# Neighbourhood projections in 512 columns, gates moved beside the first attention, queries in 512 and 256 columns

## The chip, the cores and the metric

The kernel runs on one core of a Trainium2 chip. The metric is the device time of one execution in microseconds; lower is better. The engines of the core are TensorE (PE in the views: matmuls; PEld are its weight loads), VectorE (DVE), ScalarE (ACT), GpSimd (POOL) and SyncE (SP, which here only issues loads). They run side by side, each takes its instructions in the order in which the built program holds them, and they wait for one another through semaphores.

## The reference

A trunk of two layers with shared weights over 256 context and 256 latent tokens of width 1024, all in float32. In each layer, from a normed and modulated h, one product gives everything that the two attention branches need:

```python
p = h @ w_in                       # 1024 x 4640
gate_logits, c_q, c_kv, k_r, na = p split by columns
mq = rms_norm(rms_norm(c_q) @ w_uq)          # 8 heads x 96
k_nope, mv = rms_norm(c_kv) @ w_ukv          # 8 heads x (64 + 64)
mk = rms_norm(concat(k_nope, k_r))           # 8 heads x 96
nq, nk, nv = rms_norm(na[0]), rms_norm(na[1]), na[2]   # 8 heads x 64 each
y_mla = attention(mq, mk, mv)                # dense
y_na  = attention(nq, nk, nv) over a window of the grid (with a bias) and the context
g = sigmoid(gate_logits)                     # 2 x 1024
x = x + gt1 * ((g[:1024] * (y_mla @ w_mla_o) + g[1024:] * (y_na @ w_na_o)) @ w_out)
x = x + gt2 * relu(h2 @ w_ff1)**2 @ w_ff2
```

The modulations (shift, scale and gate of both halves) are `silu(c) @ w_ada`, a product of one or two rows. In the last layer the context tokens are only needed as keys and values, so the queries and all that follows have two blocks of 128 tokens instead of four.

## The kernel before

**Products.** A float32 product is three matmuls of the type fp32r (`mm3`, L100 to L103): each operand is split into a high part and the remainder, and high·high, high·low and low·high are added in one PSUM bank. Weights come from HBM into a tile `raw` of 128 x 1024 (five buffers, `wraw`, L116 to L118, issued by SP). ScalarE copies the high part (`whi`, L130) and VectorE subtracts it for the low part (`wlo`, L131); both have three buffers. PSUM has eight banks of 512 columns, named A (two), B (three), C (two) and D (one).

**Two forms of projection.** `proj_a` has the weights stationary: 128 output columns in a pass over 512 tokens (256 in the last layer). It makes the 16 gate chunks (`gates`). `proj_b` has the activations stationary and the weights moving: N output columns for 128 tokens. It makes the queries (`w_uq`: 288, 288 and 192 columns, three, three and two heads), the keys and values (`w_ukv`, twice 512 columns) and the neighbourhood projections (`chunk_na`, two halves of 256 columns for each of keys, queries and values, two blocks of tokens in the halves of one bank A).

**The order.** The program is written in one order, and a scheduler moves instructions of each engine by their readiness and by priorities that follow the written order; what it made of it is fixed when the kernel is built. In a layer: queries, keys and values of MLA; their norms and rotary parts on GpSimd (`q_stat`, `k_stat`, `q_fin`, `k_fin`); `gates(NG0[l], "B")`, six chunks in layer 0 and eight in layer 1; then the MLA attention, head by head (`prep_mla`: transposes L780 of the queries and L785 of the keys; scores; softmax on VectorE and ScalarE; transposes of P, L871; products with the values, L886 and L891). The neighbourhood projections are written behind the MLA attention, but the scheduler runs many of their matmuls between those of the attention, where these wait for the softmax. The neighbourhood attention follows, again with matmuls of later products in between, and the rest of the gates.

**The side job.** `ada_side` works out modulations on VectorE: for each of eight k it loads a row block of `w_ada` into a `raw` tile and adds it, times one value per partition, to an accumulator of 128 x 1024 for each of two rows (L251 for the first k, L255 for the others); transposes and reductions (L266, L267) follow, and L273 on TensorE adds up the partitions. It is a generator. Each call of `step()` runs one more piece of it, and the calls stand in `proj_a` (one after each chunk), in `chunk_na` and at the ends of stages (`step(99)`, the rest). In layer 0 the accumulators of its second use (`acc_v`) are allocated under the tag "v" with one buffer, under which `mv`, the values of the MLA attention, stand too.

**The bias.** The tables of the neighbourhood bias are loaded by SP, and GpSimd adds a mask (L816). `issue_after(q_end.ins)` has it stand behind the last rotary operation of the queries.

Of the kernel before, what the change touches and what calls it, by code (L numbers as in the profile page):

```python
# [14 lines left out]
KD = 8  # L15
# [6 lines left out]
NH = 8  # L22
# [23 lines left out]
def trunk(ctx: ExitStack, tc, t):  # L46
# [10 lines left out]
    def ps(tag):  # L57
        return pp.tile([128, 512], F32, tag="ps" + tag, name="ps" + tag, bufs=BANKS[tag])
# [406 lines left out]
    for l in range(DEPTH):  # L465
# [92 lines left out]

        turn = [0]

        def proj_b(load, nk, act_h, act_l, toks, N, evac, banks=None):

            tiles = [load(i) for i in range(nk)]
            total = sum(len(x[2]) for x in tiles)
            for p0 in range(0, len(toks), 2):
                pair = toks[p0:p0 + 2]
                if banks == "one":
                    o = ps("A")
                    outs = [o[:, i * N:(i + 1) * N] for i in range(2)]
                else:  # L570
                    turn[0] += 1
                    outs = [ps(b)[:, :N] for b in (banks[p0 // 2] if banks else ("AA", "BB")[turn[0] % 2])]
                parts = [list(zip(outs, pair))] if banks != "one" else [[x] for x in zip(outs, pair)]
                for part in parts:
                    n = 0
                    for wh, wl, ks in tiles:
                        for j, k in enumerate(ks):
                            for o, tk in part:
                                cs = slice(tk * 128, (tk + 1) * 128)
                                mm3(o, act_h(k)[:, cs], act_l(k)[:, cs], wh[:, j], wl[:, j], n == 0, n == total - 1)  # L580
                            n += 1
# [136 lines left out]
            nc.gpsimd.tensor_tensor(out=krz[:, t:t + 2, :], in0=z,  # L718
                                    in1=rk[:, t:t + 2].unsqueeze(2).to_broadcast([128, 2, NH]), op=ALU.mult)

        for h0, n in ((0, 3), (3, 3), (6, 2)):
            def evac(tk, o):
                dst = mq[:, tk, h0:h0 + n, :]
                nc.scalar.activation(out=dst, in_=o.rearrange("p (h d) -> p h d", h=n), func=AF.Copy)
                head_ss(qrs[:, tk, h0:h0 + n], dst, n, QK, rq[:, tk - q0:tk - q0 + 1])
                if h0 == 6 and tk % 2:
# [21 lines left out]
        def k_fin(tk):  # L748
            z = mk[:, tk, :, 0:NOPE]
            nc.gpsimd.tensor_tensor(out=z, in0=z, in1=krz[:, tk, :].unsqueeze(2).to_broadcast([128, NH, NOPE]),  # L750
                                    op=ALU.mult)
            nc.gpsimd.tensor_tensor(out=mk[:, tk, :, NOPE:QK], in0=kr[:, tk, :].unsqueeze(1).to_broadcast([128, NH, RD]),
                                    in1=krr[:, tk, :].unsqueeze(2).to_broadcast([128, NH, RD]), op=ALU.mult)
# [41 lines left out]
        def prep_na(hp):  # L795
            cs = slice(2 * hp * HD, (2 * hp + 2) * HD)
            o = ps("C")
            for tk in range(q0, 4):
                nc.tensor.transpose(o[:, tk * 128:(tk + 1) * 128], nqk[:, tk, cs], rev if tk >= 2 else ident)
            qh, ql = qk_tile(TQ), qk_tile(TQ)  # L800
            split_ps(qh, ql, o[:, c_q], gcn[:, l:l + 1])
            o = ps("C")
            for tk in range(4):
                nc.tensor.transpose(o[:, tk * 128:(tk + 1) * 128], nqk[:, 4 + tk, cs], ident)
            kh, kl = qk_tile(), qk_tile()
            split_ps(kh, kl, o)
            biases = []
            for h in (2 * hp, 2 * hp + 1):
                bias = ap.tile([128, 2, ROWS, GW], F32, tag="bias", name="bias", bufs=3 + l)
                for row in range(ROWS):  # L810
                    src = bass.AP(tensor=t["rpb"].tensor, offset=(l * NH + h) * RPB + (7 - row) * RW + 15 - (GW - 1),
                                  ap=[[1, GW], [RW, ROWS], [1, GW]])
                    pr = (row % 2) * 64
                    nc.sync.dma_start(out=bias[pr:pr + 64, row // 2], in_=src)
                with tc.issue_after(q_end.ins):
                    nc.gpsimd.tensor_tensor(out=bias.rearrange("p a i j -> p (a i) j"),  # L816
                                            in0=bias.rearrange("p a i j -> p (a i) j"),
                                            in1=wmask.unsqueeze(1).to_broadcast([128, 2 * ROWS, GW]), op=ALU.add)
                biases.append(bias)
            return qh, ql, kh, kl, biases  # L820
# [141 lines left out]

        nrs = ap.tile([128, 8, NH], F32, name="nrs")

        def chunk_na(part, half, toks):
            def evac(tk, o):
                cs = slice(half * 256, (half + 1) * 256)
                if part == 2:
                    nc.scalar.activation(out=nv[:, tk, cs], in_=o, func=AF.Copy)
                    return  # L970
                i = 4 * part + tk
                nc.scalar.activation(out=nqk[:, i, cs], in_=o, func=AF.Copy)
                head_ss(nrs[:, i, half * 4:half * 4 + 4], nqk[:, i, cs].rearrange("p (h d) -> p h d", h=4), 4, HD)
                if half == 1:
                    fin_r(nrs[:, i, :], nrs[:, i, :], HD)
                    z = nqk[:, i, :].rearrange("p (h d) -> p h d", h=NH)
                    nc.gpsimd.tensor_tensor(out=z, in0=z, in1=nrs[:, i, :].unsqueeze(2).to_broadcast([128, NH, HD]),
                                            op=ALU.mult)
# [331 lines left out]
```

## Time and profile before

| | |
|---|---|
| median of three runs | 1305.12 us (1301.83, 1305.12, 1305.75) |
| profiled execution: time, span | 1301.52 us, 1299.7 us |
| TensorE busy | 1267.2 us, 97% |
| VectorE busy | 914.2 us, 70% |
| ScalarE busy | 582.4 us, 45% |
| GpSimd busy | 264.2 us, 20% |
| granted TensorE clock, mean | 0.997 |

The matmuls are pipelined: one is listed from its start to its modelled end, so its own duration (0.28 us for 256 columns) is longer than the time to the start of the next. What one costs is the time from start to start. The span leaves out what lies around the program (1.8 us here).

### The profile page before, as it was taken

The numbers are of one execution on the slowest core, as the hardware profiler recorded it, in microseconds if no ns is written. First come the engines' busy times: TensorE is split into PE (matmuls) and PEld (weight loads), VectorE is DVE, ScalarE is ACT, GpSimd is POOL, SyncE is SP. The second block draws the span as 40 slices with busy tenths as digits, with TensorE's granted clock in tenths as the row PEclk, the third lists the DMA queues.
The fourth block names the chain that finished last, engine by engine and source line by source line (L and its number), as shares of the span: only waits on it lengthen the run. The fifth ranks groups of instructions, "written<-read, shape, count | busy, mean of one in ns | idle before, by whom it ended". The sixth has DMA issues, their size and how long they took to land.

```text
span 1299.7 us, 20369 instructions
## 1 busy us (share of the span) xinstructions
PE 1267.2 (97%) x7831; PEld 1090.3 (84%) x7831; DVE 914.2 (70%) x1547; ACT 582.4 (45%) x1054; POOL 264.2 (20%) x258
## 2 busy tenths in 40 slices
PE   7999999999999999999999999999999989999997
PEld 5698878986787898888778888998889779999896
DVE  4558987588985579898897744766763868665553
ACT  4455277346423243422322313565663645555452
POOL 0318403401014003210201200019031112121011
PEclk9999999999999999999999999999999999999999
DMA  9855710464486326566588732487114657646652
GB/s 295 290 112 155 219 33 20 130 172 57 129 281 226 98 67 204 155 192 193 177 290 262 208 96 77 131 190 213 55 50 120 129 185 200 176 157 189 192 188 87
DMA packets 241857, 208.01 MB, mean 160 GB/s; under 512 B 24464, under 2 KB 220816, under 8 KB 241376
## 3 DMA queue, kind: packets, MB, share of 16 engines
q1 hardware_dynamic: 231728, 190.16, 50.7%
q10 hardware_dynamic: 9520, 16.29, 3.5%
q8 instruction: 61, 1.00, 0.3%
q0 software_dynamic: 512, 0.27, 0.1%
q14 instruction: 36, 0.29, 0.1%
HBM read 195.15 MB, written 11.53 MB: 159 GB/s over the span
## 4 chain that ended last, share of the span: by engine, by line
PE 52%; DVE 4%; DMA 3%; issue 2%; POOL 2%; ACT 2%; SPq 0%; POOLq 0%; ACTq 0%; DVEq 0%
PE psB L101 6%; PE psB L102 6%; PE psB L103 6%; PE psA L103 6%; PE psA L101 6%; PE psA L102 6%; PE psC L103 4%; PE psC L101 4%; PE psC L102 4%; DVE wlo L131 2%; ACT whi L130 1%; PE psD L891 1%; DMA raw<-in_w_na_o_dram 1%; PE psC L871 1%; DMA raw<-in_w_ukv_dram 1%
## 5 line engine op out<-in xcount | busy, mean ns | idle before, releaser
L131 DVE TENSOR_TENSOR wlo<-raw,whi 128x1024 fp32r<-128x1024 f32 (+3 forms) x252 | 312.2, 1240 | 171.5 <-ACT whi L130 170.5
L130 ACT ACTIVATE whi<-raw 128x1024 fp32r<-128x1024 f32 (+3 forms) x252 | 260.8, 1035 | 357.8 <-PE psB L102 98.1
L255 DVE SCALAR_TENSOR_TENSOR ada<-raw,silu,ada 128x1024 f32<-128x1024 f32 (+1 forms) x126 | 160.7, 1310 | 0.5
L101 PE MATMUL psA<-whi,h 128*128 128x256 f32 (+2 forms) x408 | 120.4, 295 | 0.5 <-ACT h L345 0.4
L103 PE MATMUL psA<-whi,h 128*128 128x256 f32 (+2 forms) x408 | 120.3, 295 | 0.0
L102 PE MATMUL psA<-wlo,h 128*128 128x256 f32 (+2 forms) x408 | 120.2, 295 | 0.0
L102 PE MATMUL psB<-h,whi 128*128 128x256 f32 (+1 forms) x272 | 91.9, 338 | 0.0
L101 PE MATMUL psB<-h,whi 128*128 128x256 f32 (+1 forms) x272 | 91.7, 338 | 0.0
L103 PE MATMUL psB<-h,wlo 128*128 128x256 f32 (+1 forms) x272 | 91.6, 337 | 0.0
L101 PE MATMUL psA<-h,whi 128*128 128x512 f32 (+1 forms) x248 | 87.6, 354 | 1.2 <-ACT h L345 1.1
L102 PE MATMUL psA<-h,whi 128*128 128x512 f32 (+1 forms) x248 | 87.3, 352 | 0.2 <-DVE h L347 0.2
L103 PE MATMUL psA<-h,wlo 128*128 128x512 f32 (+1 forms) x248 | 87.1, 351 | 0.0
L101 PEld LDWEIGHTS psA<-whi,h 128*128 128x128 f32 x408 | 77.9, 191 | 2.8 <-ACT h L345 0.9
L102 PEld LDWEIGHTS psA<-wlo,h 128*128 128x128 f32 x408 | 77.9, 191 | 2.6 <-issue 0.8
L103 PEld LDWEIGHTS psA<-whi,h 128*128 128x128 f32 x408 | 77.8, 191 | 1.9
L1163 POOL TENSOR_TENSOR h<-s,h 128x512 fp32r<-128x512 f32 (+1 forms) x32 | 38.7, 1210 | 170.7 <-ACT h L1162 153.4
L1163 POOL TENSOR_TENSOR fl<-s,fa 128x512 fp32r<-128x512 f32 (+1 forms) x32 | 35.1, 1098 | 163.9 <-ACT fa L1162 163.9
L101 PE MATMUL psB<-G,whi 128*128 128x512 f32 (+2 forms) x192 | 66.7, 347 | 0.0
L103 PE MATMUL psB<-G,wlo 128*128 128x512 f32 (+2 forms) x192 | 66.2, 345 | 0.3 <-DVE wlo L131 0.3
L102 PE MATMUL psB<-G,whi 128*128 128x512 f32 (+2 forms) x192 | 66.4, 346 | 0.0
L101 PE MATMUL psC<-G,whi 128*128 128x258 f32 (+2 forms) x200 | 62.7, 313 | 0.0
L103 PE MATMUL psC<-G,wlo 128*128 128x258 f32 (+2 forms) x200 | 62.5, 312 | 0.0
(388 smaller groups left out, 3328.6 us busy)
## 6 DMA issues: line engine op xcount, KB each, us to landing
raw<-in_w_ff_dram SPq DMA_DIRECT2D x128, 512.0 KB, 4.1
raw<-in_w_ada_dram SPq DMA_DIRECT2D x80, 512.0 KB, 4.3
raw<-in_w_in_dram SPq DMA_DIRECT2D x62, 512.0 KB, 4.2
raw<-in_w_out_dram SPq DMA_DIRECT2D x16, 512.0 KB, 5.0
spare<-in_w_ada_dram SPq DMA_DIRECT2D x12, 512.0 KB, 8.5
xT_d<-xT SPq DMA_DIRECT2D x2, 2048.0 KB, 13.2
bias<-in_rpb_dram SPq DMA_DIRECT2D x64, 64.0 KB, 7.2
g_d<-g ACTq DMA_DIRECT2D x16, 256.0 KB, 4.2
```

The costliest lines, as they stand in the source:

```text
L101: nc.tensor.matmul(out, sh, mh, start=first, stop=False)
L102: nc.tensor.matmul(out, sh, ml, start=False, stop=False)
L103: nc.tensor.matmul(out, sl, mh, start=False, stop=last)
L130: nc.scalar.activation(out=hi, in_=src, func=AF.Copy)
L131: split[:] = [nc.vector.tensor_tensor(out=lo, in0=src, in1=hi.bitcast(F32), op=ALU.subtract).ins]
L255: nc.vector.scalar_tensor_tensor(out=a, in0=raw[:, c:c + w], scalar=sc, in1=a, op0=ALU.mult, op1=ALU.add)
L871: nc.tensor.transpose(o[:, kt * 256 + i * 128:kt * 256 + (i + 1) * 128], pt[:, (kp * 2 + kt) * 128:(kp * 2 + kt + 1) * 128], perm if K == ...
L891: mm = nc.tensor.matmul(yo[z * 64:(z + 1) * 64, oc], vsel(kt, 2 * hp + z), tr[kt // 2][:, kt % 2, :], start=kt == nkt - 1, stop=kt == 0, t ...
L1163: nc.gpsimd.tensor_tensor(out=al[:, f, :], in0=s[:, :TQ], in1=ah[:, f, :].bitcast(F32), op=ALU.subtract)
```

## The change

- Gates: `NG0 = (6, 8)` becomes `NG = ((5, 5), (4, 5))`. In front of the MLA attention five chunks are written in layer 0 and four in layer 1. Five further chunks are written behind the MLA attention, ahead of the neighbourhood projections, with bank A. The last six and seven follow the neighbourhood attention.
- Neighbourhood projections: `chunk_na` has its own loop instead of `proj_b`: 512 columns in one matmul, one bank for each block of 128 tokens (A, A, B, B; for the values A, A, D, B), weight tiles of two k instead of four. In the last layer the queries come first. `step()` is called after each weight tile of the values and twice after the queries.
- Queries: 512 and 256 columns instead of 288, 288 and 192. The head that straddles the border is summed with the second part.
- The mask additions stand behind the last key operation (`k_end`) instead of the last rotary operation of the queries.

```diff
-NG0 = (6, 8)
+NG = ((5, 5), (4, 5))
...
-        for h0, n in ((0, 3), (3, 3), (6, 2)):
+        for c0, n, h0, nh, kper in ((0, 512, 0, 5, 2), (512, 256, 5, 3, 3)):
             def evac(tk, o):
...
-            proj_b(loader(t["w_uq"][l], 0, h0 * QK, n * QK, 3, 2), 2, lambda k: ch[:, k], lambda k: cl[:, k],
-                   list(range(q0, 4)), n * QK, evac)
+            proj_b(loader(t["w_uq"][l], 0, c0, n, kper, 6 // kper), 6 // kper, lambda k: ch[:, k], lambda k: cl[:, k],
+                   list(range(q0, 4)), n, evac)
...
         for tk in range(4):
-            k_fin(tk)
+            k_end = k_fin(tk)
         for tk in range(q0, 4):
-            q_end = q_fin(tk)
-
-        gates(NG0[l], "B")
+            q_fin(tk)
+
+        gates(NG[l][0], "B")
         step(99)
...
-                with tc.issue_after(q_end.ins):
+                with tc.issue_after(k_end.ins):
                     nc.gpsimd.tensor_tensor(out=bias.rearrange("p a i j -> p (a i) j"),
...
-        def chunk_na(part, half, toks):
-            def evac(tk, o):
-                cs = slice(half * 256, (half + 1) * 256)
+        def chunk_na(part, toks, banks):
+
+            outs = [ps(b) for b in banks[:len(toks)]]
+            load = loader(w_in, 0, OFF_NA + part * 512, 512, 2, 4)
+            for i in range(4):
+                wh, wl, ks = load(i)
+                for j, k in enumerate(ks):
+                    for o, tk in zip(outs, toks):
+                        cs = slice(tk * 128, (tk + 1) * 128)
+                        mm3(o, hh[:, k, cs], hl[:, k, cs], wh[:, j], wl[:, j], k == 0, k == KD - 1)
                 if part == 2:
-                    nc.scalar.activation(out=nv[:, tk, cs], in_=o, func=AF.Copy)
-                    return
+                    step()
...
-            proj_b(loader(w_in, 0, OFF_NA + part * 512 + half * 256, 256, 4, 8), 2, H, Lo, toks, 256, evac, "one")
-            if (part, half) in ((0, 1), (2, 0), (2, 1)):
+            if part == 0:
                 step(2)
...
             side.append(ada_side(((0, 4, (0, 1)), (0, 3, (0, 1))), acc_v))
-        for part in (1, 0, 2):
-            for half in range(2):
-                chunk_na(part, half, list(range(q0, 4)) if part == 0 else [0, 1, 2, 3])
+        gates(NG[l][1])
+
+        for part, banks in ((0, "AA"), (1, "AABB"), (2, "AADB")) if last else ((1, "AABB"), (0, "AABB"), (2, "AADB")):
+            chunk_na(part, list(range(q0, 4)) if part == 0 else [0, 1, 2, 3], banks)
```

The following pieces show the order of the built programs; the numbers behind the names tell tiles apart and differ between the two programs.

VectorE at the end of the MLA attention of layer 0, before. `PT` is the last tile of transposed probabilities of this attention, `nrs` the statistics of the neighbourhood projections, `ada_2976` the accumulator of the side job:

```order
351 L877 COPY PT_2435<-psC_2430 128x512
352 L606 TENSOR_REDUCE nrs_2447<-sq_2774 128x4
353 L606 TENSOR_REDUCE nrs_2447<-sq_2778 128x4
354 L131 TENSOR_TENSOR wlo_2847<-raw_2844,whi_2846 128x1024
355 L251 TENSOR_SCALAR ada_2976<-raw_2977,silu_97 128x1024
356 L606 TENSOR_REDUCE nrs_2447<-sq_2831 128x4
357 L606 TENSOR_REDUCE nrs_2447<-sq_2835 128x4
358 L251 TENSOR_SCALAR ada_2976<-raw_2977,silu_97 128x1024
359 L255 SCALAR_TENSOR_TENSOR ada_2976<-raw_2981,silu_97,ada_2976 128x1024 x2
360 L131 TENSOR_TENSOR wlo_2988<-raw_2985,whi_2987 128x1024
```

The same place afterwards (`ada_2350` is the accumulator, `wlo_2514` the low part of the first neighbourhood tile):

```order
335 L872 COPY PT_2303<-psC_2298 128x512
336 L251 TENSOR_SCALAR ada_2350<-raw_2351,silu_97 128x1024 x2
337 L255 SCALAR_TENSOR_TENSOR ada_2350<-raw_2389,silu_97,ada_2350 128x1024 x2
338 L255 SCALAR_TENSOR_TENSOR ada_2350<-raw_2427,silu_97,ada_2350 128x1024 x2
339 L255 SCALAR_TENSOR_TENSOR ada_2350<-raw_2465,silu_97,ada_2350 128x1024 x2
340 L255 SCALAR_TENSOR_TENSOR ada_2350<-raw_2503,silu_97,ada_2350 128x1024 x2
341 L131 TENSOR_TENSOR wlo_2514<-raw_2511,whi_2513 128x1024
342 L131 TENSOR_TENSOR wlo_2544<-raw_2541,whi_2543 128x1024
```

Before, splits of neighbourhood tiles stood in the attention and between the pieces of the side job; afterwards ten pieces stand in one block ahead of the first of these splits.

TensorE at the same place afterwards (`L886` is the last product with the values `mv`):

```order
990 L886 MATMUL psD_2146<-PT_2296,mv_669 64x256
991 L886 MATMUL psD_2146<-PT_2254,mv_669 64x256
992 L101 MATMUL psA_2507<-whi_2513,h_207 128x512
993 L101 MATMUL psA_2508<-whi_2513,h_207 128x512
994 L101 MATMUL psB_2509<-whi_2513,h_207 128x512
995 L101 MATMUL psB_2510<-whi_2513,h_207 128x512
996 L102 MATMUL psA_2507<-wlo_2514,h_207 128x512
997 L103 MATMUL psA_2507<-whi_2513,h_208 128x512
```

Behind the attention the first instructions are those of the first neighbourhood tile: four with its high part, then one with its low part. SP's loads for this stretch afterwards (`in_w_in` with 8x128 are gates, `in_w_ada` the side job, 2x512 the neighbourhood tiles):

```order
50 L118 DMA raw_2389<-in_w_ada_dram 128x1024
51 L118 DMA raw_2393<-in_w_in_dram 128x8x128
52 L118 DMA raw_2427<-in_w_ada_dram 128x1024
53 L118 DMA raw_2431<-in_w_in_dram 128x8x128
54 L118 DMA raw_2465<-in_w_ada_dram 128x1024
55 L118 DMA raw_2469<-in_w_in_dram 128x8x128
56 L118 DMA raw_2503<-in_w_ada_dram 128x1024
57 L118 DMA raw_2511<-in_w_in_dram 128x2x512
```

Five loads of the side job (the first, raw_2351, stands two rows above the piece) are ahead of the first neighbourhood tile, raw_2511, which takes the place of raw_2351 in SBUF.

GpSimd ahead of the MLA attention of layer 1, before (`krr` and `krz` are statistics of the keys, L750 and L752 in `k_fin` the last steps of the keys, L816 the mask additions):

```order
156 L816 TENSOR_TENSOR bias_10161<-bias_10161,wmask_73 128x512
157 L816 TENSOR_TENSOR bias_10167<-bias_10167,wmask_73 128x512
158 L816 TENSOR_TENSOR bias_10242<-bias_10242,wmask_73 128x512
159 L609 TENSOR_SCALAR qrs_8412<-qrs_8412 128x16
160 L816 TENSOR_TENSOR bias_10248<-bias_10248,wmask_73 128x512
161 L180 TENSOR_TENSOR qrs_8412<-qrs_8412,mhalf_86 128x16
162 L703 TENSOR_TENSOR qrs_8412<-qrs_8412,rt_8407 128x16
163 L716 TENSOR_TENSOR krr_8413<-krr_8413,krs_8081 128x16
```

And afterwards, the end of the keys (L745 and L747 are L750 and L752 of before, L811 is L816):

```order
171 L712 TENSOR_TENSOR krz_7992<-krr_7991,rk_7987 128x16
172 L747 TENSOR_TENSOR mqk_7656<-kr_7658,krr_7991 128x8x32
173 L745 TENSOR_TENSOR mqk_7656<-mqk_7656,krz_7992 128x8x64 x2
174 L747 TENSOR_TENSOR mqk_7656<-kr_7658,krr_7991 128x8x32
175 L811 TENSOR_TENSOR bias_9453<-bias_9453,wmask_73 128x512
176 L811 TENSOR_TENSOR bias_9459<-bias_9459,wmask_73 128x512
177 L811 TENSOR_TENSOR bias_9534<-bias_9534,wmask_73 128x512
178 L811 TENSOR_TENSOR bias_9540<-bias_9540,wmask_73 128x512
```

The four mask additions have moved from ahead of the statistics to behind the last key operation.

## Rows read from the trace of the kernel before

**Rows 1.** The page, busy time: engine, us, share of the span, instructions.

```profile
PE 1267.2 (97%) x7831; PEld 1090.3 (84%) x7831; DVE 914.2 (70%) x1547; ACT 582.4 (45%) x1054; POOL 264.2 (20%) x258
```

**Rows 2.** Windows by stage: from:to, length, busy us (instructions) of PE, PEld, DVE, ACT, POOL, PEclk, DMA.

```profile
110.60:155.50 44.90, 44.90 (x222) 38.17 (x221) 44.90 (x63) 17.57 (x30) 33.57 (x28) 1.00 0.72 221
155.50:228.00 72.50, 69.70 (x510) 58.18 (x510) 59.18 (x169) 50.57 (x118) 10.45 (x11) 1.00 0.12 35
228.00:268.00 40.00, 40.00 (x335) 39.04 (x334) 23.49 (x27) 15.94 (x31) 16.76 (x14) 1.00 0.45 136
268.00:349.00 81.00, 79.30 (x496) 56.71 (x495) 70.96 (x160) 45.35 (x107) 6.36 (x5) 1.00 0.48 102
910.00:966.00 56.00, 55.62 (x411) 47.23 (x410) 41.06 (x98) 34.67 (x77) 6.87 (x8) 1.00 0.14 41
1004.00:1055.00 51.00, 50.53 (x374) 39.88 (x374) 43.99 (x91) 29.31 (x66) 5.12 (x4) 1.00 0.58 131
```

**Rows 3.** Timeline of PE, layer 0, queries, gates, first neighbourhood matmuls: start us, us.

```profile
78.67 0.38 PE L101 MATMUL psB<-whi,G 128*128 128x288 f32 x1
...
106.24 0.42 PE L101 MATMUL psB<-whi,G 128*128 128x512 f32 x1
...
117.85 0.39 PE L101 MATMUL psB<-h,whi 128*128 128x512 f32 x1
...
149.81 0.28 PE L101 MATMUL psA<-whi,h 128*128 128x256 f32 x1
...
155.44 0.28 PE L103 MATMUL psA<-whi,h 128*128 128x256 f32 x1
155.56 0.33 PE L273 MATMUL psC<-red,m 128*128 128x64 f32 x2
```

**Rows 4.** Chain of waits, 638 to 648 us: start us, us, what.

```profile
638.20 1.82 DVE ada L251
...
640.04 4.17 DMA raw<-in_w_ff_dram
...
644.23 1.06 ACT whi L130
...
646.42 1.23 DVE wlo L131
```

**Rows 5.** Timeline of DVE: start us, us, line, operation, count.

```profile
154.06 1.24 DVE L267 TENSOR_REDUCE red<-ada 128x16 f32<-128x512 f32 x2
...
342.64 1.41 DVE L251 TENSOR_SCALAR ada<-raw,silu 128x1024 f32<-128x1024 f32 x2
...
351.05 2.48 DVE L255 SCALAR_TENSOR_TENSOR ada<-raw,silu,ada 128x1024 f32<-128x1024 f32 x2
```

**Rows 6.** Groups by line and shape of DVE, 228 to 268 us: count, busy us, mean ns.

```profile
L255 DVE SCALAR_TENSOR_TENSOR ada<-raw,silu,ada 128x1024 f32<-128x1024 f32 x10 | 12.4, 1289 | 0.0
```

**Rows 7.** Timeline of POOL, layer 1, ahead of the MLA attention.

```profile
883.31 4.80 POOL L816 TENSOR_TENSOR bias<-bias,wmask 128x512 f32<-128x512 f32 x3
...
888.48 1.30 POOL L816 TENSOR_TENSOR bias<-bias,wmask 128x512 f32<-128x512 f32 x1
...
893.23 0.21 POOL L716 TENSOR_TENSOR krr<-krr,krs 128x16 f32<-128x16 f32 x1
...
910.38 0.61 POOL L752 TENSOR_TENSOR mqk<-kr,krr 128x256 f32<-128x256 f32 x1
```

**Rows 8.** Timeline of PE, layer 1, first transposes of the MLA attention.

```profile
910.00 0.38 PE L780 MATMUL psC<-ident,mqk 128*96 128x128 f32 x2
...
911.05 0.32 PE L785 MATMUL psC<-ident,mqk 128*96 128x128 f32 x1 [0.34 <-POOL mqk L752]
```

**Rows 9.** Windows around an idle stretch of PE in layer 1.

```profile
1060.50:1064.00 3.50, 1.17 (x8) 0.77 (x7) 2.01 (x2) 2.57 (x4) 2.45 (x4) 1.00 0.34 120
1064.00:1067.40 3.40, 3.40 (x16) 3.40 (x17) 1.75 (x2) 1.22 (x2) 0.43 (x1) 0.50 0.88 276
1067.40:1072.00 4.60, 4.00 (x34) 3.79 (x32) 1.88 (x4) 1.20 (x2) 1.27 (x2) 1.00 1.00 318
```

More of the change, by code (lines that the diff above doesn't have):

```diff
@@ L559, in trunk, with proj_b @@
         turn = [0]
-        def proj_b(load, nk, act_h, act_l, toks, N, evac, banks=None):
+        def proj_b(load, nk, act_h, act_l, toks, N, evac):
             tiles = [load(i) for i in range(nk)]
@@ L566, in proj_b @@
                 pair = toks[p0:p0 + 2]
[L567 to L581, printed above, removed]
+                turn[0] += 1
+                outs = [ps(b)[:, :N] for b in ("AA", "BB")[turn[0] % 2]]
+                n = 0
+                for wh, wl, ks in tiles:
+                    for j, k in enumerate(ks):
+                        for o, tk in zip(outs, pair):
+                            cs = slice(tk * 128, (tk + 1) * 128)
+                            mm3(o, act_h(k)[:, cs], act_l(k)[:, cs], wh[:, j], wl[:, j], n == 0, n == total - 1)
+                        n += 1
                 for o, tk in zip(outs, pair):
@@ L719, in k_stat @@
                                     in1=rk[:, t:t + 2].unsqueeze(2).to_broadcast([128, 2, NH]), op=ALU.mult)
-        for h0, n in ((0, 3), (3, 3), (6, 2)):
+        for c0, n, h0, nh, kper in ((0, 512, 0, 5, 2), (512, 256, 5, 3, 3)):
             def evac(tk, o):
[L723 to L726, printed above, removed]
+                flat = mq[:, tk].rearrange("p h d -> p (h d)")
+                nc.scalar.activation(out=flat[:, c0:c0 + n], in_=o, func=AF.Copy)
+                head_ss(qrs[:, tk, h0:h0 + nh], mq[:, tk, h0:h0 + nh, :], nh, QK, rq[:, tk - q0:tk - q0 + 1])
+                if c0 and tk % 2:
                     q_stat(tk - 1)
-            proj_b(loader(t["w_uq"][l], 0, h0 * QK, n * QK, 3, 2), 2, lambda k: ch[:, k], lambda k: cl[:, k],
-                   list(range(q0, 4)), n * QK, evac)
+            proj_b(loader(t["w_uq"][l], 0, c0, n, kper, 6 // kper), 6 // kper, lambda k: ch[:, k], lambda k: cl[:, k],
+                   list(range(q0, 4)), n, evac)
         for hf in range(2):
@@ L751, in k_fin @@
                                     op=ALU.mult)
-            nc.gpsimd.tensor_tensor(out=mk[:, tk, :, NOPE:QK], in0=kr[:, tk, :].unsqueeze(1).to_broadcast([128, NH, RD]),
+            return nc.gpsimd.tensor_tensor(out=mk[:, tk, :, NOPE:QK], in0=kr[:, tk, :].unsqueeze(1).to_broadcast([128, NH, RD]),
                                     in1=krr[:, tk, :].unsqueeze(2).to_broadcast([128, NH, RD]), op=ALU.mult)
         for tk in range(4):
-            k_fin(tk)
+            k_end = k_fin(tk)
         for tk in range(q0, 4):
-            q_end = q_fin(tk)
-        gates(NG0[l], "B")
+            q_fin(tk)
+        gates(NG[l][0], "B")
         step(99)
@@ L963, in trunk @@
         nrs = ap.tile([128, 8, NH], F32, name="nrs")
-        def chunk_na(part, half, toks):
-            def evac(tk, o):
-                cs = slice(half * 256, (half + 1) * 256)
-                if part == 2:
-                    nc.scalar.activation(out=nv[:, tk, cs], in_=o, func=AF.Copy)
-                    return
-                i = 4 * part + tk
[L972 to L978, printed above, removed]
-            proj_b(loader(w_in, 0, OFF_NA + part * 512 + half * 256, 256, 4, 8), 2, H, Lo, toks, 256, evac, "one")
-            if (part, half) in ((0, 1), (2, 0), (2, 1)):
+        def chunk_na(part, toks, banks):
[3 more added lines that the diff above has]
+                wh, wl, ks = load(i)
+                for j, k in enumerate(ks):
+                    for o, tk in zip(outs, toks):
+                        cs = slice(tk * 128, (tk + 1) * 128)
+                        mm3(o, hh[:, k, cs], hl[:, k, cs], wh[:, j], wl[:, j], k == 0, k == KD - 1)
+                if part == 2:
+                    step()
+            for o, tk in zip(outs, toks):
+                if part == 2:
+                    nc.scalar.activation(out=nv[:, tk], in_=o, func=AF.Copy)
+                    continue
+                i = 4 * part + tk
+                z = nqk[:, i, :].rearrange("p (h d) -> p h d", h=NH)
+                nc.scalar.activation(out=nqk[:, i], in_=o, func=AF.Copy)
+                head_ss(nrs[:, i, :], z, NH, HD)
+                fin_r(nrs[:, i, :], nrs[:, i, :], HD)
+                nc.gpsimd.tensor_tensor(out=z, in0=z, in1=nrs[:, i, :].unsqueeze(2).to_broadcast([128, NH, HD]),
+                                        op=ALU.mult)
+            if part == 0:
                 step(2)
```

## The prediction

> **What bounds the kernel now.** I read the busy lines first: TensorE is busy 97% of the span, VectorE 70% [rows 1]. So time is saved only by issuing fewer or denser matmuls, or lost by making TensorE wait. The windows by stage, read second, show where it is close to waiting [rows 2]. Ahead of the first layer's MLA attention (110.6 to 155.5 us) VectorE is busy for the whole 44.90 us, and TensorE too: the two are level. From 228 to 268 us (neighbourhood projections) TensorE is busy all 40.00 us and VectorE only 23.49: here VectorE has room. The four attention windows leave TensorE idle for 2.8, 1.7, 0.4 and 0.5 us. The timelines, read last, give the durations.
>
> The sum is made against the profiled execution: span 1299.7 us, time 1301.52 us, 3.6 us below the median 1305.12 of the runs shown (1301.83 to 1305.75).
>
> **Fewer matmuls.** From 117.85 to 149.81 us stand 141 gate matmuls of 512 columns start to start, 0.2267 us each; from 149.81 to 155.44 us 47 of 256 columns, 0.1198 us each [rows 3]. Two of 256 cost 0.2396, so one of 512 in their place saves 0.0129 us. The neighbourhood projections fall from 8 k x 4 tokens x 3 products x 6 halves = 576 to 288 in layer 0 (3.7 us) and from 480 to 240 in layer 1, where the queries have two tokens (3.1 us): 6.8 us together. The query projection of layer 0 runs from 78.67 to 106.24 us, 27.57 us for 216 matmuls [rows 3]. Afterwards it has 72 of 512 and 72 of 256 columns: 16.3 + 8.6 = 24.9 us. That would save 2.6; I take 2.2, since some of the 27.57 is starting up, and half of it, 1.1, in layer 1 with half the tokens. All matmul savings: 10.1 us (bounds 8 to 11).
>
> What weighs on this: the start-to-start time in the rows grows by 0.1069 us from 256 to 512 columns, which leaves 0.0129 us per matmul that doesn't depend on the columns. The Trainium skill (TensorE: Matmul & The Clock Gate, section "Wait — 56ns, not 53.3ns?") gives columns over 2.4 GHz plus about 2.5 ns, which would be an estimated 109 and 216 ns. By that rule all 636 matmuls saved are worth 636 x 0.0025 = 1.6 us, and the sum would be 8.5 us higher. The rows show 119.8 and 226.7 ns for these fp32r products, so the trace disagrees and I go by the rows.
>
> **The end of the first attention in layer 0 (the largest term).** The five new gates beside this attention each call step(), which issues pieces of the adaLN side job. Its accumulator shares its only buffer with mv, the values of this very attention, so its first VectorE operation (L251) can't start before the last product with mv. The order shows the rest. On VectorE ten operations of the side job (two L251, eight L255) stand in one block behind the last PT copy, and L131 for the first neighbourhood tile comes after all ten. On TensorE the last eight L886 are followed by four matmuls that need only the high half of that tile, and then by ones that need its low half; nothing else is there to run. On SP five side-job loads stand ahead of the tile, and the tile's load goes into the buffer that the first side-job load occupies, so it is not even issued until the two L251 are done.
>
> The trace of before has such a chain elsewhere: L251 (1.82 us), then a load into raw (4.17 us), whi (1.06 us), wlo (1.23 us), one behind the other [rows 4]. Here: two L251 take 1.41 us, two L255 2.48 us [rows 5], so ten take 1.41 + 4 x 2.48 = 11.33 us, and L131 adds 1.23 [rows 4]: 12.6 us. The load path is shorter (1.41 + 4.17 + 1.06 = 6.6 us) and doesn't decide; it lets four matmuls run, 4 x 0.2267 = 0.9 us. With some 0.3 us for the hand-overs TensorE idles 12.0 us. Bounds: 10.5 if hand-overs cost nothing and a few operations run faster, 14.5 with L255 at its mean of 1.289 [rows 6] and each L251 at 1.82 [rows 4]. In before the same ten ran inside 228 to 268 us, where L255 has ten operations in 12.4 us [rows 6], at no cost, because TensorE was busy 40.00 of 40.00 [rows 2]. So the whole 12.0 is a loss.
>
> **The wait ahead of the attention in layer 0.** The reduced modulations come out of VectorE at 154.06 + 1.24 = 155.30 and TensorE reads them at 155.56 [rows 3, 5], with no idle time. Afterwards TensorE has one 512-column gate less (24 x 0.2267 = 5.4 us) and 26 new gate matmuls (5.9) where 48 of 256 columns stood (5.7), and queries 2.2 shorter: it arrives at 155.56 - 2.2 - 5.2 = 148.1. VectorE loses one split (1.2 us) and starts up to 2.2 us earlier: it ends at 151.9 to 154.1. TensorE waits 3.8 to 6.0 us; the lower bound is 1, if its small operations run faster with less beside them. I take 3.8.
>
> **The wait ahead of the attention in layer 1.** The key transposes (L780, L785) need the last key operation of GpSimd, whose chain ends at 910.38 + 0.61 = 910.99 us [rows 7]. TensorE comes at 910.00 and waits 0.34 us before its last transpose [rows 8], because eight gates (192 matmuls, 23.0 us) cover the chain. Two things change. The bias additions (4.80 + 1.30 us, rows 7) now stand behind the last key operation, so the chain ends 6.1 us earlier, at 904.9, or 904.4 with the queries 1.1 us shorter, as the second half of the keys has its own floor (bounds 903.5 to 905.8). And only four gates remain in front: TensorE is there at 910.00 - 1.1 - 96 x 0.1198 = 897.4. It waits about 7 us; the gates taken away return beside the attentions, so all but the former 0.34 is lost: +6.6 (bounds 4 to 8.5). The bias additions behind the keys are hidden: the neighbourhood scores that need them start in the window from 1004 us [rows 2].
>
> **The clock after a wait.** From 1060.5 to 1064 us TensorE is busy for 1.17 of 3.5 us; in the following 3.4 us the granted clock is 0.50, the 1.2 GHz level, and 16 matmuls start, against 34 in the 4.6 us behind them at 1.00 [rows 9]. That is 1.7 us lost. I count it for the two long waits (3.4 us), not for the one of 3.8 (upper bound 5.1 for three).
>
> **The attention windows.** The MLA windows lose evacuations, squares and statistics of the neighbourhood chunks and gain five gate evacuations of each layer. The order has about as much filler there as before in matmul time. Idle time that could go is 2.8 us in the first and 0.4 in the second [rows 2], and some slack hidden in matmuls that wait in the pipeline: I take -3.5. The neighbourhood window of layer 0 holds VectorE to 70.96 of 81.00 us [rows 2] and gets about eight L255 more (10 us), since the side job is later than before; it comes to about 81 of 81: I take +1.5, bounds -1 to +5. Together -2 (bounds -8 to +5).
>
> **Sum:** -10.1 + 12.0 + 3.8 + 6.6 + 3.4 - 2 = +13.7 us. From the profiled execution that is 1315.2, from the median 1318.8. I forecast 1317, with its own range 1311 to 1323.
>
> **Rivals.**
>
> A. Faster: TensorE, at 97%, is the only thing that decides, and the two long waits don't arise: the pieces of the side job run when VectorE is idle anyway, and the shorter GpSimd chain arrives with the gates. Then only -10.1 and -2 count: 1289.5 to 1293, say 1292. For it speaks that before has next to no idle time at these places and that VectorE is 70% busy over the span. Against it: VectorE takes its instructions in the order written, and L131 stands behind the ten. To be measurably faster it needs all waits and clock losses, 25.8 us in the sum, to fall below 8 us.
>
> B. One long wait instead of two: the wait in layer 1 is short, because the statistics of GpSimd (L180, part of the 17.75 us from 893.23 to 910.99, rows 7) run faster without bias additions and with less work beside them. Without 6.6 and one clock loss: +5.4, so 1307 to 1310.5, say 1309. Against it, the chain would have to shrink by another 7 us.
>
> C. More is lost: the neighbourhood window of layer 0 becomes bound by VectorE (+5 instead of +1.5), the wait ahead of the first attention costs 6.0 and a third clock loss: +7.4 on the sum, 1324.
>
> D. The gain per merged matmul is small, as the page's rule has it (above): the same waits and 8.5 us more, 1325. The gaps of 0.1198 and 0.2267 us in the rows of this kernel speak against it.
>
> **How the numbers follow.** The chances: forecast 0.58, A 0.09, B 0.18, C 0.12, D 0.03. A measurement of this kernel can't tell less than about 0.3% (3.9 us) from no change, so "same" is 1301.2 to 1309.0. Faster: A, 0.08. Same: the lower half of B and what of A meets one of the two waits, 0.10. Slower: 0.82. The range for 8 in 10 takes in most of B below and C above: 1306.5 to 1326.
>
> **What will show it right or wrong.** In the profile of the changed kernel: an idle gap of 10 to 14.5 us on TensorE after the last product of the first attention, ended by wlo (L131), with ten operations of L251 and L255 back to back on VectorE and the granted clock at 0.50 behind it; a gap of 4 to 8.5 us before L775 or L780 in layer 1, ended by GpSimd (L747); 1 to 6 us before L273 in layer 0, ended by VectorE; 512-column neighbourhood matmuls at 0.227 us start to start. The forecast fails if the first of these gaps is under 6 us, or if the attention windows shorten by more than 10 us together.

## The result and the profile after

| | before | after |
|---|---|---|
| median | 1303.47 us (1301.13 to 1305.75, 4 runs) | 1316.32 us (1315.06 to 1316.49, 4 runs) |
| span of the profiled execution | 1299.7 us | 1314.4 us |
| mean granted TensorE clock | 0.997 | 0.987 |

The ratio is 1.0097 (95% interval 1.0074 to 1.0119): the change makes the kernel about 1% slower, with 1316.32 us where 1317 were forecast. The profiled execution took 1316.18 us.

The busy line of the page (engine, us, share, instructions; it answers to [rows 1]):

```profile
PE 1266.3 (96%) x7195; PEld 1057.7 (80%) x7195; DVE 913.0 (69%) x1525; ACT 578.5 (44%) x1004; POOL 264.2 (20%) x258
```

TensorE has 636 matmuls fewer and is busy for about as long, in a longer span. Where it waited is in its timeline. These five are the waits at the places that the prediction spoke of; the bracket at the end gives the idle time before the instruction and what ended it (the last two answer to [rows 8]):

```profile
147.84 0.79 PE L103 MATMUL psA<-h,wlo 128*128 128x512 f32 x1 [5.04 <-DVE wlo L131]
...
234.58 0.79 PE L101 MATMUL psA<-whi,h 128*128 128x512 f32 x1 [6.02 <-ACT whi L130]
...
240.78 0.79 PE L102 MATMUL psA<-wlo,h 128*128 128x512 f32 x1 [4.13 <-DVE wlo L131]
...
910.74 0.31 PE L780 MATMUL psC<-ident,mqk 128*96 128x128 f32 x1 [3.61 <-POOL mqk L745]
...
912.32 0.45 PE L780 MATMUL psC<-ident,mqk 128*96 128x128 f32 x1 [1.26 <-POOL mqk L747]
```

That is 5.0 us ahead of the first attention of layer 0, 10.2 us behind it, and 4.9 us ahead of the first attention of layer 1. In the course of each the granted clock falls to 0.50, and the stretch at half the clock lasts on behind it. The windows (length, busy us and instructions of PE, PEld, DVE, ACT, POOL, then the granted clock; they answer to [rows 2]):

```profile
146.48:153.30 6.82, 5.46 (x13) 4.30 (x14) 6.82 (x11) 1.49 (x2) 0.00 (x0) 0.50 0.96 303
156.16:228.19 72.03, 70.94 (x448) 54.04 (x447) 53.42 (x159) 47.04 (x106) 0.00 (x0) 1.00 0.12 41
228.19:231.80 3.61, 0.38 (x4) 0.00 (x0) 3.19 (x4) 2.51 (x2) 0.00 (x0) 1.00 0.18 37
231.80:245.47 13.67, 6.76 (x15) 4.88 (x16) 11.20 (x10) 3.17 (x3) 0.00 (x0) 0.50 0.79 244
245.47:307.65 62.18, 62.18 (x277) 51.47 (x276) 36.88 (x37) 21.75 (x30) 30.41 (x24) 1.00 0.46 138
307.65:385.92 78.27, 77.47 (x467) 53.11 (x466) 73.21 (x158) 45.84 (x105) 7.22 (x5) 1.00 0.52 122
911.07:917.89 6.82, 5.57 (x24) 5.23 (x25) 1.17 (x2) 1.07 (x2) 6.14 (x6) 0.50 0.13 46
```

To add waits and slow stretches up, I take for each stretch its length less what its matmuls need at the start-to-start times of undisturbed rows (0.2267 us for 512 columns, 0.1198 for 256, and so on). This "excess" is what TensorE lost there:

| stretch (us) | before | after | side_spread | combined_a | combined_b |
|---|---|---|---|---|---|
| layer 0: gates to the first transposes | 0.0 | 7.9 | 7.3 | 0.3 | 0.3 |
| MLA attention | 8.1 | 5.2 | 4.2 | 4.4 | 4.4 |
| neighbourhood projections | 0.4 | 13.8 | 0.4 | 0.4 | 0.4 |
| neighbourhood attention | 4.0 | 3.4 | 3.4 | 4.6 | 4.0 |
| gates, output projections | 3.7 | 2.9 | 3.7 | 4.2 | 4.2 |
| layer 1: queries, keys | 2.3 | 0.3 | 0.3 | 0.3 | 0.3 |
| MLA attention | 2.8 | 9.9 | 9.3 | 3.5 | 3.5 |
| neighbourhood attention | 2.1 | 3.3 | 2.5 | 5.6 | 2.7 |
| output projections | 6.3 | 7.4 | 7.5 | 7.8 | 4.8 |

(The last three columns are experiments, below.) From before to after these nine rows grow by 24.4 us; the span grew by 14.7. The difference of the two, 9.7 us, is what the matmuls themselves became shorter. So the saving that the change was worth is there, and two and a half times as much was lost in waits and at half clock.

### The profile page after: what moved, and what is told of

Same layout as the page of the kernel before. It is cut to its first block, busy times and chain, and to the rows that moved or that the text cites. A ratio compares the mean times of both kernels' runs of the same rounds, so it can differ in the third digit from the quotient of the medians.

```text
span 1314.4 us, 18982 instructions
## 1 busy us (share of the span) xinstructions
PE 1266.3 (96%) x7195; PEld 1057.7 (80%) x7195; DVE 913.0 (69%) x1525; ACT 578.5 (44%) x1004; POOL 264.2 (20%) x258
## 4 chain that ended last, share of the span: by engine, by line
PE 53%; DVE 4%; DMA 2%; issue 2%; ACT 1%; POOL 1%; POOLq 0%; SPq 0%; ACTq 0%; DVEq 0%
PE psB L101 7%; PE psB L102 7%; PE psB L103 7%; PE psA L101 6%; PE psA L103 6%; PE psA L102 6%; PE psC L103 4%; PE psC L101 4%; PE psC L102 4%; DVE wlo L131 1%; ACT whi L130 1%; PE psD L886 1%; DMA raw<-in_w_mla_o_dram 1%; PE psC L866 1%; DMA bias<-in_rpb_dram 1%
## 5 line engine op out<-in xcount | busy, mean ns | idle before, releaser
L131 DVE TENSOR_TENSOR wlo<-raw,whi 128x1024 fp32r<-128x1024 f32 (+3 forms) x250 | 308.4, 1236 | 175.8 <-ACT whi L130 175.0
L255 DVE SCALAR_TENSOR_TENSOR ada<-raw,silu,ada 128x1024 f32<-128x1024 f32 (+1 forms) x126 | 164.7, 1340 | 0.6 <-DVE ada L255 0.2
L103 PE MATMUL psA<-h,wlo 128*128 128x512 f32 (+1 forms) x288 | 102.1, 355 | 5.0 <-DVE wlo L131 5.0
L101 PE MATMUL psA<-h,whi 128*128 128x512 f32 (+1 forms) x288 | 102.6, 357 | 1.2 <-ACT h L345 1.1
L102 PE MATMUL psA<-h,whi 128*128 128x512 f32 (+1 forms) x288 | 102.5, 356 | 0.2 <-DVE h L347 0.2
L102 PE MATMUL psB<-h,whi 128*128 128x512 f32 (+1 forms) x232 | 79.7, 344 | 0.0
L101 PE MATMUL psB<-h,whi 128*128 128x512 f32 (+1 forms) x232 | 79.5, 344 | 0.0
L103 PE MATMUL psB<-h,wlo 128*128 128x512 f32 (+1 forms) x232 | 79.5, 342 | 0.0
L103 PEld LDWEIGHTS psA<-h,wlo 128*128 128x128 f32 x288 | 55.9, 194 | 12.0 <-DVE wlo L131 5.5
L101 PE MATMUL psA<-whi,h 128*128 128x512 f32 (+1 forms) x152 | 58.2, 384 | 6.5 <-ACT whi L130 6.0
L101 PEld LDWEIGHTS psA<-h,whi 128*128 128x128 f32 x288 | 56.0, 195 | 8.9 <-ACT h L345 1.8
L101 PE MATMUL psC<-G,whi 128*128 128x258 f32 (+2 forms) x200 | 62.7, 314 | 0.0
L102 PE MATMUL psC<-G,whi 128*128 128x258 f32 (+2 forms) x200 | 62.5, 312 | 0.0
L102 PE MATMUL psA<-wlo,h 128*128 128x512 f32 (+1 forms) x152 | 58.3, 383 | 4.1 <-DVE wlo L131 4.1
L102 PEld LDWEIGHTS psA<-h,whi 128*128 128x128 f32 x288 | 56.0, 194 | 6.7 <-DVE h L347 0.8
```

What stands on the lines that cost most here:

```text
L131: split[:] = [nc.vector.tensor_tensor(out=lo, in0=src, in1=hi.bitcast(F32), op=ALU.subtract).ins]
L255: nc.vector.scalar_tensor_tensor(out=a, in0=raw[:, c:c + w], scalar=sc, in1=a, op0=ALU.mult, op1=ALU.add)
```

## The experiments

Eight kernels in two sets; each set shared its runs of the kernel before, whose median was 1301.56 us in the first and 1302.89 in the second. Times are compared by their ratio to these. By its ratio of 1.0097 the changed kernel would have been at 1314.2 in the first set.

**side_behind_gates.** The second use of the side job is registered behind the five gates instead of ahead of them:

```diff
+        gates(NG[l][1])
         if l == 0:
...
             side.append(ada_side(((0, 4, (0, 1)), (0, 3, (0, 1))), acc_v))
-        gates(NG[l][1])
```

> The changed kernel with the second use of the side job registered behind the five gates beside the first attention, so that these gates no longer step it; nothing else changed. Theory (the ten accumulations ahead of the first neighbourhood split hold TensorE): the gap of 6.02 + 4.13 us behind the first attention of layer 0 goes and with it the half clock behind it (13.9 us of excess there becomes under 2). But the accumulations are owed: 15 of them and 8 transposes and reductions now stand on VectorE behind the neighbourhood attention with no gate left to cover them, some 15 x 1.28 + 8 x 0.62 = 24 us, of which the last products of the attention hide a few; a new gap of 15 to 20 us there ended by VectorE. Sum 1316 - 14 + 18 = about 1320. Rival 1 (the gap is the load and split of the first 512-column tile, whatever the side job does): gap stays, 1316. Rival 2 (the owed work is hidden by the out projections): 1303.

Measured: 1318.65 us, ratio 1.013 (1.0111 to 1.015). The theory holds, against both rivals: the excess of the neighbourhood projections fell from 13.8 to 0.2 us, and that of gates and output projections in layer 0 rose from 2.9 to 18.8. VectorE's timeline behind the neighbourhood attention, TensorE's two longest waits there, and the two windows over this place, the second of them at half clock:

```profile
370.98 12.04 DVE L255 SCALAR_TENSOR_TENSOR ada<-raw,silu,ada 128x1024 f32<-128x1024 f32 x10
```
```profile
379.58 0.80 PE L101 MATMUL psB<-ym,whi 128*128 128x512 f32 x1 [5.53 <-ACT whi L130]
...
387.82 0.48 PE L273 MATMUL psC<-red,m 128*128 128x64 f32 x1 [3.16 <-DVE red L267]
```
```profile
365.40:376.19 10.79, 8.65 (x41) 6.67 (x37) 10.72 (x15) 1.79 (x3) 0.00 (x0) 1.00 0.70 209
376.19:396.67 20.48, 11.30 (x24) 7.39 (x25) 18.39 (x26) 3.17 (x3) 0.00 (x0) 0.50 0.84 297
```

The side job is a debt: taken from one place without being paid elsewhere, it stops TensorE at the next place that has to wait for it. Here that is not only a split (1.21 us of wait ended by wlo): 5.53 and 1.27 us were ended by whi, whose load had come late, and 3.16 us by the side job's own last reduction.

**side_spread.** In addition, more calls of step() between the weight tiles:

```diff
-                if part == 2:
+                if part != 1 or i > 1:
                     step()
```

> As side_behind_gates, and the side job is stepped after the weight tiles of all neighbourhood parts from the third tile on (ten steps in place of four), so that VectorE does two accumulations between two splits while TensorE has 5.4 us of matmuls per tile. Theory: the 13.9 us of excess behind the first attention of layer 0 falls under 3 us and no new gap comes behind the neighbourhood attention: 1316 - 12 = 1304 (1301 to 1307). Rival (VectorE's room is used up, 12 splits and 22 accumulations are 43 us in a stretch of 65): gaps before wlo in the projections of 5 us or more together, 1309 to 1312.

Measured: 1302.53 us, ratio 1.0008 (0.9999 to 1.0017), 11.6 us below the changed kernel by the ratios. The 13.8 us are gone (0.4) and nothing came in their place. VectorE's timeline of this kernel at the start of the projections shows why: a split, two accumulations, a split, two accumulations. Before each split it is VectorE that waits, for whi:

```profile
234.72 1.23 DVE L131 TENSOR_TENSOR wlo<-raw,whi 128x1024 fp32r<-128x1024 f32 x1 [2.16 <-ACT whi L130]
235.86 2.47 DVE L255 SCALAR_TENSOR_TENSOR ada<-raw,silu,ada 128x1024 f32<-128x1024 f32 x2
239.70 1.23 DVE L131 TENSOR_TENSOR wlo<-raw,whi 128x1024 fp32r<-128x1024 f32 x1 [1.37 <-ACT whi L130]
240.84 2.48 DVE L255 SCALAR_TENSOR_TENSOR ada<-raw,silu,ada 128x1024 f32<-128x1024 f32 x2
```

**eight_gates_layer1.**

```diff
-NG = ((5, 5), (4, 5))
+NG = ((5, 5), (8, 5))
```

> The changed kernel with eight gates instead of four in front of the MLA attention of layer 1 (then five, then three). Theory (the gap of 3.61 + 1.26 us before the key transposes is GpSimd's chain, uncovered because four gates take 11.5 us less): the gap goes and the half clock of 6.8 us behind it (3.4 us lost), so 8 us less there, excess of the first attention of layer 1 from 10.0 to about 3. The neighbourhood attention of layer 1 loses 96 matmuls of filler (11.5 us) and may wait 2 to 4 us more: 1316 - 8 + 3 = 1311. Rival (the gap is a price of the new filler, not of the chain): excess unchanged, 1316 or more.

Measured: 1318.78 us, ratio 1.0133 (1.0115 to 1.0151). The mechanism was as expected and the sum was not. The wait before the key transposes went (the first attention's excess fell from 9.9 to 3.5 us), but the neighbourhood attention of layer 1 rose from 3.3 to 13.2, where I had allowed 2 to 4 us. The 96 matmuls taken from it are 11.5 us, and 9.9 of that came back as waits and a half-clock stretch of 13.7 us. TensorE's timeline and windows there:

```profile
1046.56 0.44 PE L866 MATMUL psC<-rev,P 128*128 128x128 f32 x2 [2.06 <-DVE P L836]
...
1057.30 0.48 PE L866 MATMUL psC<-rev,P 128*128 128x128 f32 x1 [2.78 <-DVE qk L766]
```
```profile
1023.40:1056.30 32.90, 28.54 (x200) 20.83 (x198) 29.22 (x61) 19.45 (x45) 3.84 (x3) 1.00 0.56 102
1056.30:1069.96 13.66, 12.30 (x47) 7.31 (x48) 10.72 (x24) 5.61 (x15) 1.27 (x1) 0.50 0.05 17
```

A gate is worth its length wherever TensorE would wait. There are sixteen in a layer, and the new projections serve less as filler beside the MLA attention of layer 1 than the halves of bank A did: 41 of their matmuls run there (9.3 us), where 181 of 256 columns ran before (21.7 us).

**mask_behind_queries.**

```diff
-            q_fin(tk)
+            q_end = q_fin(tk)
...
-                with tc.issue_after(k_end.ins):
+                with tc.issue_after(q_end.ins):
```

> The changed kernel with the mask additions of the bias back behind the last rotary operation of the queries, as before. Theory (GpSimd's chain decides the start of the first attention in layer 1): the additions (4.99 us in one block after the change, 6.10 before) are in the chain again, the gap grows from 4.9 to about 10.5 us, 1316 + 5.5 = 1321.5. Rival (the additions ran in time that GpSimd was waiting anyway, as it does for krr in 1.1 us of the chain): 1317 or less.

Measured: 1320.56 us, ratio 1.014 (1.0124 to 1.0157). Layer 1 went the way of the theory: the waits before the key transposes grew from 4.9 to 9.1 us (the two of layer 1 below are the last of four), the excess from 9.9 to 14.3. What I had not expected is layer 0: the wait of 5.04 us ahead of its first attention became 1.62 and 2.20, the excess fell from 7.9 to 4.4. So the match with the expected 1321.5 is luck: these two places add up to 0.9 us, while the span grew by 4.1 (1318.5 against 1314.4). Another 1.4 stand in the output projections of layer 1; for the rest no one place can be named.

```profile
145.28 0.50 PE L103 MATMUL psA<-h,wlo 128*128 128x512 f32 x1 [1.62 <-DVE wlo L131]
...
153.23 0.43 PE L273 MATMUL psC<-red,m 128*128 128x64 f32 x2 [2.20 <-DVE red L267]
...
913.84 0.45 PE L780 MATMUL psC<-ident,mqk 128*96 128x128 f32 x1 [5.00 <-POOL mqk L745]
...
915.41 0.45 PE L780 MATMUL psC<-ident,mqk 128*96 128x128 f32 x1 [1.13 <-POOL mqk L747]
```

The groups of VectorE by line and shape, 100 to 160 us, first of the changed kernel and then of this one (count, busy us, mean ns):

```profile
L255 DVE SCALAR_TENSOR_TENSOR ada<-raw,silu,ada 128x512 f32<-128x512 f32 x28 | 25.9, 987 | 0.0
```
```profile
L255 DVE SCALAR_TENSOR_TENSOR ada<-raw,silu,ada 128x512 f32<-128x512 f32 x28 | 21.7, 835 | 0.0
```

The 28 accumulations take 4.2 us more when the mask additions and the second half of the key operations of GpSimd fall beside their last sixteen. The trace also tells which operations of GpSimd do it. In the changed kernel three accumulations run beside the mask additions (137.6 to 142.5 us) and the next six (142.7 to 146.4 us) beside nothing:

```profile
L255 DVE SCALAR_TENSOR_TENSOR ada<-raw,silu,ada 128x512 f32<-128x512 f32 x3 | 5.2, 1775 | 0.0
```
```profile
L255 DVE SCALAR_TENSOR_TENSOR ada<-raw,silu,ada 128x512 f32<-128x512 f32 x6 | 4.1, 739 | 0.0
```

Beside the key multiplications of 512 columns (L745) one takes 1.53 us, beside L180, which has 16 columns, 0.74 as beside nothing. Of the 4.2 us, 1.9 come from the mask additions and 2.3 from the second half of the key operations, which in mask_behind_queries start only at 145.27 us, behind the whole row of accumulations.

**mask_only.** The kernel before with the additions behind the keys:

```diff
-                with tc.issue_after(q_end.ins):
+                with tc.issue_after(k_end.ins):
```

> The kernel before with the mask additions behind the last key operation and nothing else of the change. Theory (in layer 0 the additions, moved beside VectorE's long row of accumulations, slow that row, as between the changed kernel and mask_behind_queries, where the mean of the 512-column L255 is 987 and 835 ns): L255 there from 937 to above 950 ns, and since TensorE has no slack ahead of the first attention, +1 to +4 us; layer 1 gains its 0.3 us wait at most. Rival (the additions are off every path): within 0.5 us.

Measured: 1305.44 us, ratio 1.0018 (1.0009 to 1.0027): +2.4 us, so the rival's half microsecond is out and the theory's range holds. Its route is shown for a part only: in the profiled run the mean of L255 rose from 937 to 959 ns, 0.6 us in all, and the excess ahead of the first attention by 1.3. Two further stretches in layer 0, the MLA attention and the output projections, were 1.5 us longer each, at half clock in 177.8 to 181.2 and 403.1 to 406.5 us. The waits at these places (1.34 and 0.51 us, 1.04 and 0.98) stand in the kernel before too, just as long, and there the clock stayed at 1.00; why it fell here is open. Over the ten runs the mean granted clock lies between 0.993 and 0.998, so how much of the 2.4 us is due to the additions is not shown.

**queries_only.** The kernel before with the queries' loop of the change:

```diff
-        for h0, n in ((0, 3), (3, 3), (6, 2)):
+        for c0, n, h0, nh, kper in ((0, 512, 0, 5, 2), (512, 256, 5, 3, 3)):
...
```

> The kernel before with the queries in 512 and 256 columns and nothing else of the change. By the start-to-start times of the traces (0.2267 us for 512 columns, 0.1198 for 256, 27.57 us for the 216 matmuls of before) the query projection is 2.0 us shorter in layer 0 and 1.0 in layer 1: -3.0 us. But what follows decides whether it is kept: ahead of the first attention of layer 0 VectorE is busy throughout, so there some of the 2.0 may turn into a wait (then -1 to -2). By the rule of columns over 2.4 GHz plus 2.5 ns: -0.3 us.

(The last figure is an estimate by the rule of the Trainium skill that the prediction weighs: TensorE: Matmul & The Clock Gate, section "Wait — 56ns, not 53.3ns?".)

Measured: 1298.37 us, ratio 0.9965 (0.9953 to 0.9977): -4.5 us, more than the -3.0 by start-to-start times, and far from the -0.3 of that rule; the trace disagrees with it for these products. Layer 0 gave its 2.0 us (first query matmul to the first of the keys: 80.93 to 106.47 us in this kernel, 25.54 against 27.57 in [rows 3]):

```profile
80.93 0.47 PE L101 MATMUL psB<-whi,G 128*128 128x512 f32 x1
...
106.47 0.40 PE L101 MATMUL psB<-whi,G 128*128 128x512 f32 x1
```

In layer 1 queries and keys together took 24.0 us instead of 27.1: 1.0 by the matmuls, and 2.0 of excess that went, since the wait of 1.6 us for an evacuation of the values (mv) between them is gone.

**combined_a.** side_spread, the mask additions behind the queries in layer 0 and behind the keys in layer 1, and other numbers of gates:

```diff
-NG = ((5, 5), (4, 5))
+NG = ((6, 5), (6, 4))
...
-                with tc.issue_after(k_end.ins):
+                with tc.issue_after((k_end if last else q_end).ins):
```

> side_spread with the mask additions behind the queries in layer 0 and behind the keys in layer 1, six gates in front in layer 0 (then five, five) and six in layer 1 (then four, six). Theory: against side_spread (1302.5) the wait ahead of the first attention of layer 0 loses 3.5 us by the mask and most of the rest (3.8 of 7.3 us excess) by the sixth gate, the wait of 4.7 us and its half clock in layer 1 go with two gates more (23.9 less filler there): -6.4, and the neighbourhood attentions, with 24 filler matmuls less each, lose about 1 and 2.5 us: 1302.5 - 3.5 - 3 - 6.4 + 3.5 = 1293. Rival (every gate moved in front is missed behind, as eight_gates_layer1 showed with -6.4 and +9.9): 1299 or more.

Measured: 1294.03 us, ratio 0.9928 (0.9916 to 0.994), 0.7% faster than the kernel before and faster than the changed one, and 1 us above the sum. Ahead of the first attention of layer 0 no wait is left (excess 0.3), and two gates in front are nearly all that layer 1 needed there (9.3 to 3.5), at 3.1 us in its neighbourhood attention.

**combined_b.** The same in layer 0; in layer 1 the projections as before and the gates 8, 0 and 8:

```diff
+        if last:
+            for part in (1, 0, 2):
+                for half in range(2):
+                    chunk_na256(part, half, list(range(q0, 4)) if part == 0 else [0, 1, 2, 3])
+        else:
...
```

> As combined_a in layer 0; in layer 1 the neighbourhood projections as before the change (256 columns in halves of bank A, beside the MLA attention) and eight gates in front, eight behind. Theory: layer 1 has the excess of before (2.8, 0.3, 2.1, 6.3 us in its four stretches, against 9.3, 0.4, 2.5, 7.5 in side_spread), and its projections cost 2.9 us more: 8 - 2.9 = 5 us better than side_spread in layer 1, 5.5 in layer 0: 1292. If the gates of layer 1 in front of the attention matter more than the width of the matmuls, this is level with or below combined_a; if the width matters more, it is above it by 2 us or more.

Measured: 1292.74 us, ratio 0.9923 (0.991 to 0.9937), the lowest median, but level with combined_a, whose interval overlaps. In layer 1 no gain of the wider matmuls is seen: they save 3.1 us there (240 x 0.0129), and the excess of the four rows of layer 1 is 17.2 us in combined_a against 11.3 in combined_b. Since the numbers of gates differ as well, the two are not told apart. Span and mean granted clock of the core in combined_b:

```profile
core 0: 1288.1 us, clock 0.998
```

The width of the projections is thus not what made the change slow: combined_a has the wide form in both layers.

## Why the prediction was right

The forecast of 1317 met 1316.32. Its terms add up to +13.7 us; measured in the same way they are -9.7 + 13.4 + 7.9 + 7.1 - 4.0 = +14.7. The mechanism was right at the two long waits and only in part at the third, ahead of the first attention in layer 0; that the sum came so close is partly luck: one term was 4.1 us too small, and three others together 3.5 too large. Step by step:

- **Fewer matmuls, -10.1 us.** About -9.7 by the table. Counted from the rows it is 9.8: 528 x 0.0129 = 6.8 us for the projections, and 2.0 and 1.0 for the queries (queries_only). Start to start 512 columns take 0.2267 us in the new projections too: from the first to the second of these rows of the changed kernel stand 159 matmuls in 36.04 us.

```profile
262.59 0.39 PE L101 MATMUL psB<-whi,h 128*128 128x512 f32 x1
...
298.63 0.39 PE L101 MATMUL psB<-whi,h 128*128 128x512 f32 x1
```

- **The end of the first attention, +12.0 and a clock loss of 1.7.** Excess +13.4. The wait was 6.02 + 4.13 = 10.15 and the rest, 3.3 us, is the half clock: the two parts were off by somewhat under 2 us in opposite directions. VectorE's timeline, the ten operations ahead of the split (it answers to [rows 5]):

```profile
228.61 1.41 DVE L251 TENSOR_SCALAR ada<-raw,silu 128x1024 f32<-128x1024 f32 x2 [2.05 <-PE psD L886]
229.94 9.65 DVE L255 SCALAR_TENSOR_TENSOR ada<-raw,silu,ada 128x1024 f32<-128x1024 f32 x8
239.51 3.49 DVE L131 TENSOR_TENSOR wlo<-raw,whi 128x1024 fp32r<-128x1024 f32 x3
```

  The ten take 228.61 to 239.51 = 10.9 us, where 11.3 were summed: in one row eight L255 take 9.65 us, 1.21 each from start to start. The load path ended the first part of the wait (whi was done 5.9 us after the first L251 began, where 6.6 were summed), but as forecast it doesn't decide: the split of the tile starts when the ten are done. And the four matmuls with the high part ran at half clock and took 2.1 us, longer than the 0.9 subtracted. side_behind_gates and side_spread show that the ten are the cause.
- **Ahead of the first attention in layer 0, +3.8 us.** Measured +7.9: this term was mis-sized, beyond its bound of 6.0. VectorE's timeline of the changed kernel:

```profile
137.50 9.15 DVE L255 SCALAR_TENSOR_TENSOR ada<-raw,silu,ada 128x512 f32<-128x512 f32 x9
146.57 2.35 DVE L131 TENSOR_TENSOR wlo<-raw,whi 128x1024 fp32r<-128x1024 f32 x2
...
152.43 1.23 DVE L267 TENSOR_REDUCE red<-ada 128x16 f32<-128x512 f32 x2
```

  VectorE ended at 153.66 us, within the 151.9 to 154.1 that were reckoned. But TensorE stopped before that, at the low part of the filler gate, whose split (L131, 146.57) stands behind a row of sixteen accumulations (the last nine are shown). The gate's tile was late for the same reason: SP had waited 5.2 us for an accumulation to give a buffer back before it could issue the load at 139.30 us. So 24 of the 26 filler matmuls, which I had let run while VectorE finished, came after the wait, thirteen of them at half clock (5.46 us in the window 146.48 to 153.30, 2.95 at full clock, a loss of 2.5 that I had left out for this wait), and the transposes came only at 156.16 us. The mask additions have a part in it. I had called them hidden in layer 1 and put them at nothing in layer 0; with them behind the queries the stop ended at 145.28, was 1.62 us long, and the excess was 3.5 us smaller (mask_behind_queries).
- **Ahead of the first attention in layer 1, +6.6 and 1.7.** Excess +7.1: a wait of 4.87 and the rest at half clock (6.82 us long). GpSimd's chain ended at 911.64 + 0.62 = 912.26 us (its timeline, below; it answers to [rows 7]), 41.3 us after the first query matmul of the layer (871.0), against 51.1 in before (859.9): 9.8 us earlier, not 6.6, since the additions had taken 6.1 us and the keys came 3 us sooner; TensorE came 14.6 us earlier, not 12.6, for the same 2 us in queries and keys.

```profile
911.64 0.62 POOL L747 TENSOR_TENSOR mqk<-kr,krr 128x256 f32<-128x256 f32 x1
```

- **The attention windows, -2.** MLA -2.9 in layer 0; neighbourhood -0.6 and +1.2, output projections -0.8 and +1.1, keys of layer 1 -2.0: together -4. The neighbourhood window of layer 0 did not become bound by VectorE (73.21 of 78.27 us busy).

Of the rivals, A (no waits) and D (little gain per matmul) are out by the rows above. B (one wait) and C (about 1324) had their parts: the loss in layer 1 was 1.2 us smaller, the one ahead of the attention in layer 0 4.1 us larger with a clock loss of its own, and with the 2 us more that the attention windows gave they nearly cancelled.

## What to carry to other kernels

Work that is queued by a generator beside other work lands where its operands come free, and everything behind it on that engine waits: look at which buffer it shares with whom, and spread it where the engine has room between the splits that feed TensorE (side_spread). Filler for TensorE is a fixed stock; before moving it from one gap to another, price the gap that it leaves. A wait of TensorE costs more than its length: here waits of 5.04, 10.15 and 4.87 us went with an excess of 7.9, 13.4 and 7.1.

## What was not expected of the hardware

The clock: with waits of 5.04 and 4.87 us the granted clock was 0.50 in stretches of 6.82 us, where before a shorter one (2.3 us of idle, [rows 9]) had been followed by 3.40; and in mask_only it fell at waits of 0.5 to 1.3 us that had left it at 1.00 in the kernel before. These stretches are seen, not explained. VectorE beside GpSimd: one accumulation of 512 columns takes 0.74 us beside nothing or beside L180, 1.53 beside a key multiplication and 1.78 beside a mask addition, so the same 28 took 21.7 us in one order and 25.9 in another.
